# New VectorE durations in the table that paces a hybrid decoder layer's background work

## The chip, the cores and the metric

One core of a Trainium2 chip runs the whole program. The metric is device microseconds (us): the median of three runs of the kernel before is 3039.61 us (3038.51 to 3039.74). A difference under 0.2%, some 6 us, can't be told from no change.

## The reference

One layer of a hybrid decoder over 1024 prompt tokens, and the same layer for one token of each of 8 samples, 2048 wide:

```
h = RMSNorm(x) * (1 + scale(c)) + shift(c)
P = h @ W_in                                  # u, z_s5, r, k, v, w, a, z_rw, two gates
o_s5: S5, 64 groups of 64 complex states:  X_t = a * X_{t-1} + B u_t ;  y = Re(C X) + D u
      y = gelu(y);  o_s5 = y * sigmoid(y @ w_glu + b_glu) * silu(z_s5)
o_rw: 16 heads of 64, a matrix state S:
      S = S * diag(decay) - (S kk) b^T + v k^T ;  o = S r
      o = groupnorm(o) + (r . k * r_k) v ;  o_rw = o * silu(z_rw)
mixed = sigmoid(g_s5) * (o_s5 @ W_out[:1024]) + sigmoid(g_rw) * (o_rw @ W_out[1024:])
x = x + gate(c) * mixed;  y = RMSNorm(x)
```

## The kernel before

**Foreground.** The large products are a list of jobs of 128 output rows. A job of W_in has 3 groups of columns of 48 matmuls each (16 blocks of the contraction, three f16 products for each, L453), 144 in all. Each group fills one of three PSUM buffers (pg) and is evacuated by VectorE: by L517 for r, k, v and w, by L553 for z_s5, by L568 for z_rw. The jobs stand in this order: eight for u, eight for z_s5, then w and a, then k, v, r and z_rw of a pair of heads, for eight pairs, with three jobs for the output gates between one pair's r and its z_rw, and at the end the rest of the gates, the GLU and the 16 output jobs. From the second pair on a turn is seven jobs: k, v, r, three gate jobs, z_rw.

**Background.** The rest is written as generators that stand in a list: the weights' scaling and splitting into two f16 parts (L157, L403, L404), the S5 system (L1127 to L1310), and for each pair of heads
- *operands* (rw_job, L651 to L742): elementwise work, and last eight blocks of masked products, each of 8 matmuls L737 and of four VectorE instructions L739 to L742, a *set* below; then they write to dA in DRAM;
- *inverse* (tinv): dA is loaded, 63 steps of two VectorE instructions each (L798, L800), and the result goes through DRAM to TT;
- *chain*: 16 steps, one after the other, of 7 matmuls: L826, L827, L837 for the inputs, then L834, then L839 and L840; between them XS (L828), UB (L835), S (L842) and ON (L845) on VectorE;
- *tail* (L861 to L157 omx): groupnorm and gate of the chain's output, and the write to od. It needs Z, which the pair's z_rw job fills.

**What sets the order.** Each generator yields three numbers with every step: VectorE ns, TensorE ns and a gap until it is due again. Driver keeps two clocks, pe and ve. After every 8 large matmuls, and after every evacuation, slot() advances pe by these and ve by what the evacuation returned, and lets a generator step while it is due and ve is at most 800 ns ahead of pe, six times at most. Larger numbers thus put fewer steps between the same large matmuls. Where a job needs something that isn't emitted yet, force() emits all that is missing at once, with no large matmul between: job.need for z_rw (it needs the chain and the tail of the pair before), the S5 system ahead of the w job, and the last chain ahead of the first job behind the pairs. A list scheduler then places the emitted instructions on each engine, and may pull large matmuls that are ready a little forward. An engine runs its instructions in that order.

## Time and profile before

| what | value |
|---|---|
| median of three runs | 3039.61 us |
| profiled execution | 3042.96 us, its span 3041.2 us |
| mean granted TensorE clock | 0.959 of full speed |
| TensorE (PE) matmuls busy | 2743.5 us, 90% of the span |
| VectorE (DVE) busy | 2028.4 us, 67%, 4892 instructions |
| ScalarE (ACT), GpSimd (POOL) busy | 984.4 us (32%), 461.2 us (15%) |
| chain that ended last | PE 40%, DVE 28%, DMA 19%, ACT 4% |

PE's busy time is of pipelined matmuls whose ends are modelled. The 2743.5 us leave 297.7 us in which no matmul runs. The inverses of the eight pairs begin at 797.4, 999.7, 1197.1, 1407.9, 1617.0, 1824.1, 2032.3 and 2244.1 us.

### The profile page before, as it was taken

How to read it: one execution, taken by the hardware profiler on the slowest of the kernel's cores; microseconds unless marked ns; L12 is line 12 of the kernel's file. 1: busy time of each engine (PE TensorE's matmuls, PEld its weight loads, DVE VectorE, ACT ScalarE, POOL GpSimd, SP SyncE). 2: the span in 40 equal slices, each digit the busy share in tenths (PEclk: the TensorE clock that was granted, in tenths of full speed). 3: DMA queues.
4: the chain of work that ended last, by engine and by line, in shares of the span. 5: the costliest groups of instructions: out<-in, count | busy, mean ns of one | idle time of the engine just before them, and what ended most of it. 6: DMA issues, size and time to landing. Idle time of an engine off the chain costs nothing.

```text
span 3041.2 us, 47546 instructions
## 1 busy us (share of the span) xinstructions
PE 2743.5 (90%) x18330; PEld 1819.4 (60%) x18330; DVE 2028.4 (67%) x4892; ACT 984.4 (32%) x1734; POOL 461.2 (15%) x749
## 2 busy tenths in 40 slices
PE   5699998999989999899899998998998985899997
PEld 1166666666656666566576675665665653566665
DVE  5579878744675766867767658568566495655555
ACT  2143213324342243243242332432431132422321
POOL 2100000010111112121021111111210222111213
PEclk6799999999999999999999999999999997999998
DMA  9734343331321223213212231232133163664453
GB/s 337 257 80 97 73 86 79 89 97 43 68 66 47 64 67 78 63 51 75 59 52 75 53 81 55 57 78 68 45 80 80 45 210 120 206 203 135 133 146 126
DMA packets 434163, 298.38 MB, mean 98 GB/s; under 512 B 115120, under 2 KB 400464, under 8 KB 432656
## 3 DMA queue, kind: packets, MB, share of 16 engines
q1 hardware_dynamic: 397648, 277.71, 32.9%
q10 hardware_dynamic: 36128, 17.33, 2.1%
q8 instruction: 144, 2.36, 0.3%
q14 instruction: 83, 0.68, 0.1%
q0 software_dynamic: 160, 0.30, 0.0%
HBM read 241.93 MB, written 53.35 MB: 97 GB/s over the span
## 4 chain that ended last, share of the span: by engine, by line
PE 40%; DVE 28%; DMA 19%; ACT 4%; issue 4%; POOL 2%; SPq 1%; ACTq 0%; POOLq 0%; DVEq 0%
PE pg L453 28%; DMA ws<-w_in 7%; DVE TM L798 4%; DVE ZB L800 4%; DMA od<-BV 4%; DVE wlo L404 3%; DVE wam L157 3%; DMA wa<-w_ada 3%; DMA sg<-sgd 2%; PE pma L737 2%; PE up L840 1%; ACT whi L403 1%; PE sp L839 1%; PE up L834 1%; PE pmod L236 1%
## 5 line engine op out<-in xcount | busy, mean ns | idle before, releaser
L453 PEld LDWEIGHTS <-whi 128*128 128x128 f16 x9600 | 943.8, 99 | 571.5 <-issue 109.1
L453 PE MATMUL pg<-H,whi 128*128 128x344 f16 (+2 forms) x3840 | 1200.6, 313 | 66.6 <-DVE ZB L517 38.3
L453 PE MATMUL pg<-H,wlo 128*128 128x344 f16 (+2 forms) x3840 | 1200.9, 313 | 0.0
L453 PE MATMUL pg<-HL,whi 128*128 128x344 f16 (+2 forms) x3840 | 1200.3, 313 | 0.0
L453 PEld LDWEIGHTS <-wlo 128*128 128x128 f16 x4800 | 475.4, 99 | 243.2 <-issue 16.9
L403 ACT ACTIVATE whi<-ws,wsc 128x512 f16<-128x512 f32 x404 | 265.8, 713 | 490.0 <-DVE wsc L150 268.9
L157 DVE TENSOR_REDUCE wam<-ws 128x1 f32<-128x512 f32 x404 | 266.8, 680 | 157.5 <-DMA ws<-w_in 106.5
L404 DVE SCALAR_TENSOR_TENSOR wlo<-ws,wsc,whi 128x512 f16<-128x512 f32 x404 | 301.7, 776 | 57.5 <-ACT whi L403 54.3
L453 PE MATMUL pg<-OH,whi 128*128 128x344 f16 (+3 forms) x960 | 301.0, 314 | 22.0 <-ACT whi L403 10.2
L453 PE MATMUL pg<-OLo,whi 128*128 128x344 f16 (+3 forms) x960 | 301.1, 314 | 3.2 <-DVE OLo L1422 3.2
L453 PE MATMUL pg<-OH,wlo 128*128 128x344 f16 (+3 forms) x960 | 300.9, 313 | 1.0 <-DVE wlo L404 1.0
L798 DVE TENSOR_TENSOR TM<-ZB 128x252 f32<-128x252 f32 (+52 forms) x504 | 179.0, 355 | 88.2 <-DMA ZB<-c_t 77.9
L800 DVE TENSOR_TENSOR ZB<-ZB,TM 128x252 f32<-128x252 f32 (+52 forms) x504 | 179.8, 357 | 10.5
L154 POOL PARTITION_ALL_REDUCE wg<-wm x105 | 50.3, 480 | 865.2 <-DVE wm L157 422.7
L831 POOL TENSOR_SCALAR SG<-S,GC 128x128 f32<-128x128 f32 x120 | 98.6, 821 | 358.5 <-DVE S L842 221.7
L829 ACT COPY XR<-xp 64x128 f32<-64x128 f32 x128 | 33.1, 259 | 351.4 <-DVE XS L828 335.1
L236 PE MATMUL pmod<-wa,cs 128*32 128x512 f32 x256 | 76.7, 866 | 39.1 <-DMA wa<-w_ada 27.6
L842 DVE SCALAR_TENSOR_TENSOR S<-sp,GC,SG 128x128 f32<-128x128 f32 x120 | 41.6, 347 | 73.5 <-POOL SG L831 38.1
L1505 DVE SCALAR_TENSOR_TENSOR sg<-pg,oinv,sg 128x344 f32<-128x344 f32 (+3 forms) x96 | 54.8, 571 | 47.6 <-PE pg L453 47.5
L701 ACT COPY BT<-ZB 64x128 f32<-64x128 f32 x256 | 75.3, 296 | 33.6 <-PE pma L737 24.3
L834 PE MATMUL up<-XS,TT 128*128 128x128 f32 x256 | 56.7, 304 | 30.8 <-DMA TT<-dT 16.9
L147 DVE TENSOR_SCALAR p2m<-wg 128x1 f32<-128x1 f32 x105 | 15.9, 151 | 102.0 <-POOL wg L154 101.1
(443 smaller groups left out, 3223.0 us busy)
## 6 DMA issues: line engine op xcount, KB each, us to landing
ws<-w_in SPq DMA_DIRECT2D x162, 512.0 KB
wa<-w_ada SPq DMA_DIRECT2D x64, 512.0 KB
sg<-sgd SPq DMA_DIRECT2D x32, 516.0 KB
gw<-w_ada ACTq DMA_DIRECT2D x32, 512.0 KB
ws<-w_out SPq DMA_DIRECT2D x32, 512.0 KB
XT<-xT SPq DMA_DIRECT2D x16, 516.0 KB
xo<-xT SPq DMA_DIRECT2D x16, 516.0 KB
ZB<-dA SPq DMA_DIRECT2D x8, 1024.0 KB
```

The lines of the kernel that those rows point to most:

```text
L157: self.nc.vector.tensor_reduce(out=out, in_=in_, axis=axis, op=ALU.max, apply_absolute_value=True)
L236: self.nc.tensor.matmul(q[s:s + 32], cs[:, kt, :], w[:, i, :], start=(kt < 4), stop=(kt >= 12))
L403: nc.scalar.activation(out=hi[:, ks, :], in_=s, func=AF.Copy, scale=job.sc[:, 0, 0:1])
L404: nc.vector.scalar_tensor_tensor(out=lo[:, ks, :], in0=s, scalar=job.sc[:, 0, 0:1], in1=hi[:, ks, :], op0=ALU.mult, op1=ALU.subtract)
L453: nc.tensor.matmul(q[:, :w], a[:, wk, :], b[:, rk, g0:g1], start=(n == 0), stop=(n == tot - 1))
L701: self.nc.scalar.copy(self.BT[k % 2][i][64 * h:64 * h + 64, :, 64 * h:64 * h + 64], t[64 * h:64 * h + 64, 128 * k:128 * k + 128].rearrange ...
L737: nc.tensor.matmul(q[:, e, 128 * i:128 * i + 128], w[:, e, :], self.AR[:, a, 128 * e:128 * e + 128], start=True, stop=True)
L798: nc.vector.tensor_tensor(out=TM, in0=row.unsqueeze(1).to_broadcast([128, n, m]), in1=TL[:, :n, k:k + 1].to_broadcast([128, n, m]), op=ALU ...
L800: nc.vector.tensor_tensor(out=TL[:, :n, k + 1:], in0=TL[:, :n, k + 1:], in1=TM, op=ALU.subtract)
L831: nc.gpsimd.tensor_scalar(out=self.SG, in0=S0, scalar1=g, scalar2=None, op0=ALU.mult)
L834: nc.tensor.matmul(up[:, 0, :], self.TT[:, a, :], xs, start=True, stop=True)
L1505: V.scalar_tensor_tensor(out=f, in0=q[:, :g1 - g0], scalar=job.inv[:, w:w + 1], in1=f, op0=ALU.mult, op1=ALU.mult)
```

## The change

Only the numbers that generators yield and evacuations return are changed, most of them upward. No instruction is added, removed or changed. The core of the diff, with the lines that follow it named in words:

```diff
@@ weights: one block of the split (a scan 600 -> 715, the scale 300 -> 790)
-                yield (620, 0, 0)
+                yield (785, 0, 0)
@@ evacuations: L517 (z_s5 900 -> 1150, z_rw 450 -> 605)
-            return 450.0
+            return 610.0 + (255.0 if g1 == NC else 0.0)
@@ operands: a set of masked products (elementwise steps 1150 -> 1260 to 1440)
-            yield (840, 872, 0)
+            yield (1280, 872, 0)
@@ inverse: one of 63 steps
-            yield (2 * (66 + n * m) / 0.96, 0, 0)
+            yield (2 * (200.0 + n * m), 0, 0)
@@ chain: three yields of one of 16 steps
-            yield (200, 436, CG[0])
+            yield (325, 436, CG[0])
...
-            yield (200, 436, CG[1])
+            yield (325, 436, CG[1])
...
-            yield (400, 436, CG[2])
+            yield (710, 436, CG[2])
@@ tail: half of the groupnorm's scale (other steps 600 to 1200 -> 720 to 1410)
-                yield (680, 872, 0)
+                yield (1030, 872, 0)
@@ S5: powers, runs (1600 -> 2830), fix (2000 -> 2500), scan (560 -> 1220), out (1200 -> 1320)
-        yield (1150, 0, 0)
+        yield (167 + 136 * nt, 0, 0)
```

Three places show what this moves. The first is VectorE's order at the end of the z_rw job of the third turn (job 36), before. Here the masked sets are done; L883 (behind them), L886 and omx are the tail, L798 and L800 the next inverse, and the last row is the first evacuation of z_rw.

```order
L763 STREAM_TRANSPOSE ON<-ZB 128x1024
L886 SCALAR_TENSOR_TENSOR BV<-BV,c_vec,Z 128x1024
L404 SCALAR_TENSOR_TENSOR wlo<-ws,wsc,whi 128x512
L157 TENSOR_REDUCE omx<-BV 128x1
L404 SCALAR_TENSOR_TENSOR wlo<-ws,wsc,whi 128x512 x2
L798 TENSOR_TENSOR TM<-ZB 128x63
L404 SCALAR_TENSOR_TENSOR wlo<-ws,wsc,whi 128x512
L800 TENSOR_TENSOR ZB<-ZB,TM 128x63
L763 STREAM_TRANSPOSE ON<-ZB 128x1024
L798 TENSOR_TENSOR TM<-ZB 128x62
L800 TENSOR_TENSOR ZB<-ZB,TM 128x62
L568 SCALAR_TENSOR_TENSOR Z<-pg,winv,Z 128x344
```

The same place on VectorE in the changed kernel, from the tail's L886 on:

```order
L886 SCALAR_TENSOR_TENSOR BV<-BV,c_vec,Z 128x1024
L739 TENSOR_TENSOR ZB<-pma,c_mat 128x64
L740 TENSOR_TENSOR ZB<-pma,c_mat 128x64
L741 TENSOR_TENSOR M<-pma,c_mat 128x192
L742 TENSOR_TENSOR M<-pma,c_mat 128x192
L157 TENSOR_REDUCE omx<-BV 128x1
L568 SCALAR_TENSOR_TENSOR Z<-pg,winv,Z 128x344 x3
L763 STREAM_TRANSPOSE BV<-ZB 128x1024
L763 STREAM_TRANSPOSE ON<-ZB 128x1024
```

The sets have moved behind the chain's end and into the tail, seven of them after the chain's last instruction (L845), and all three evacuations of z_rw stand behind them.

The second place is TensorE's order at the masked products (L737) of the same turn, before; L453 rows are large matmuls and their weight loads.

```order
L737 MATMUL pma<-AR,BT_5261 128x128
L737 MATMUL pma<-AR,BT_5262 128x128 x2
L737 MATMUL pma<-AR,BT_5261 128x128
L453 LDWEIGHTS whi
L453 MATMUL pg<-HL,whi 128x344
L737 MATMUL pma<-AR,BT_5263 128x128
L737 MATMUL pma<-AR,BT_5264 128x128 x2
L737 MATMUL pma<-AR,BT_5263 128x128
L453 LDWEIGHTS wlo
L453 MATMUL pg<-H,wlo 128x344
```

In the changed kernel they stand between two groups, with the tail's L880 and the next operands' L651, and the last rows are the next job's first large matmul:

```order
L880 MATMUL pmo<-c_mat,ON 128x128 x4
L737 MATMUL pma<-AR,BT_5261 128x128
L737 MATMUL pma<-AR,BT_5262 128x128 x2
L737 MATMUL pma<-AR,BT_5261 128x128
L737 MATMUL pma<-AR,BT_5263 128x128
L737 MATMUL pma<-AR,BT_5264 128x128 x2
L737 MATMUL pma<-AR,BT_5263 128x128
L651 MATMUL pml<-LW,LW_5275 128x344 x2
L453 LDWEIGHTS whi
L453 MATMUL pg<-H,whi 128x347
```

In that run of instructions stand 28 L737, 8 L880, 3 L778 and 2 L651, and no large matmul.

The third place is TensorE's order at the end of the last chain, before: one step with large matmuls between its parts.

```order
L834 MATMUL up<-XS_5269,TT 128x128
L453 LDWEIGHTS whi
L453 MATMUL pg<-HL,whi 128x344
L453 LDWEIGHTS wlo
L453 MATMUL pg<-H,wlo 128x344
L453 LDWEIGHTS whi
L453 MATMUL pg<-H,whi 128x344
L839 MATMUL sp<-UB,BN 128x128
L840 MATMUL up<-UB,M 64x128
L453 LDWEIGHTS whi
L453 MATMUL pg<-HL,whi 128x344
```

In the changed kernel, up to the first large matmul of the job behind the pairs:

```order
L826 MATMUL xp<-S_5266,AR 128x128
L827 MATMUL xp<-VN,M 128x128
L837 MATMUL sp<-VN,KN 128x128
L834 MATMUL up<-XS_5269,TT 128x128
L839 MATMUL sp<-UB,BN 128x128
L840 MATMUL up<-UB,M 64x128
L880 MATMUL pmo<-c_mat,ON 128x128 x8
L453 LDWEIGHTS whi
L453 MATMUL pg<-H,whi 128x344
```

Six steps of the chain stand so, without a large matmul between, and the tail's L880 follow at once.

## Rows read from the trace of the kernel before

**Rows 1.** Windows by stage: length, busy PE, PEld, DVE, ACT, POOL, PEclk, DMA share, GB/s

```profile
174.30:716.50 542.20, 508.47 (x3457) 352.94 (x3457) 392.78 (x883) 164.84 (x275) 34.47 (x80) 0.97 0.37 86
...
966.10:2227.90 1261.80, 1180.67 (x7807) 804.98 (x7805) 872.96 (x2294) 437.99 (x847) 209.47 (x370) 0.99 0.25 64
2227.90:2433.90 206.00, 184.07 (x1238) 124.31 (x1236) 123.10 (x325) 45.96 (x88) 27.49 (x41) 0.97 0.26 69
2433.90:2600.00 166.10, 125.72 (x861) 81.61 (x861) 120.06 (x190) 54.07 (x79) 37.49 (x33) 0.87 0.50 161
```

**Rows 2.** Windows of one turn, from one inverse's start to the next's

```profile
1617.00:1688.00 71.00, 63.80 (x423) 41.75 (x421) 64.24 (x180) 15.81 (x29) 8.45 (x22) 1.00 0.17 48
1688.00:1701.10 13.10, 8.58 (x58) 5.31 (x56) 7.10 (x13) 5.64 (x11) 1.08 (x5) 0.99 0.79 161
1701.10:1785.90 84.80, 83.68 (x539) 57.76 (x540) 52.15 (x127) 34.83 (x61) 16.55 (x27) 0.98 0.18 51
1785.90:1798.50 12.60, 12.45 (x96) 10.11 (x96) 10.27 (x43) 7.88 (x26) 1.72 (x4) 1.00 0.06 19
1798.50:1824.10 25.60, 25.60 (x180) 17.52 (x178) 10.62 (x16) 7.77 (x13) 6.03 (x4) 1.00 0.54 126
```

**Rows 3.** Waits of PE, whole span: waiting line, releaser, us, times, longest

```profile
PE pg L453 <- DVE ZB L517: 38.3, 24, 3.6
...
PE pg L453 <- DVE Z L568: 14.4, 9, 3.5
```

**Rows 4.** Groups of VectorE instructions, 1590 to 1830 us: busy, mean ns, idle before

```profile
L404 DVE SCALAR_TENSOR_TENSOR wlo<-ws,wsc,whi 128x512 f16<-128x512 f32 x32 | 23.9, 768 | 4.6 <-ACT whi L403 4.6
L800 DVE TENSOR_TENSOR ZB<-ZB,TM 128x204 f32<-128x204 f32 (+31 forms) x65 | 23.6, 363 | 1.3
...
L883 DVE SCALAR_TENSOR_TENSOR BV<-pmo,c_vec,BV 128x256 f32<-128x256 f32 x8 | 3.3, 479 | 5.4 <-PE pmo L880 5.4
L741 DVE TENSOR_TENSOR M<-pma,c_mat 128x192 f32<-128x192 f32 x9 | 3.1, 348 | 0.0
...
L869 DVE TENSOR_REDUCE gvr<-pmq 128x8 f32<-128x512 f32 x4 | 2.7, 686 | 0.3
L886 DVE SCALAR_TENSOR_TENSOR BV<-BV,c_vec,Z 128x1024 f32<-128x1024 f32 x2 | 2.5, 1244 | 0.0
...
L739 DVE TENSOR_TENSOR ZB<-pma,c_mat 128x64 f32<-128x64 f32 x9 | 2.0, 223 | 2.3 <-PE pma L737 2.3
```

**Rows 5.** Groups of PE instructions, 1785.9 to 1798.5 us, columns as above

```profile
L737 PE MATMUL pma<-AR,BT 128*128 128x128 f32 x64 | 8.7, 282 | 0.1
```

**Rows 6.** Timeline of PE, one step of the last chain: start, length, instruction

```profile
2408.04 0.38 PE L834 MATMUL up<-XS,TT 128*128 128x128 f32 x2
...
2408.80 0.49 PE L839 MATMUL sp<-UB,BN 128*128 128x128 f32 x2
...
2409.59 0.32 PE L453 MATMUL pg<-HL,whi 128*128 128x344 f16 x1
...
2410.04 0.31 PE L453 MATMUL pg<-HL,whi 128*128 128x344 f16 x1
2410.18 0.38 PE L826 MATMUL xp<-S,AR 128*128 128x128 f32 x2
...
2411.18 0.49 PE L834 MATMUL up<-XS,TT 128*128 128x128 f32 x2
```

**Rows 7.** Timeline of VectorE, the same step

```profile
2409.40 0.35 DVE L842 SCALAR_TENSOR_TENSOR S<-sp,GC,SG 128x128 f32<-128x128 f32 x1 [0.65 <-PE sp L839]
```

**Rows 8.** GpSimd's part of the tail, first lines on the line L872

```profile
L872 POOL TENSOR_TENSOR gvr<-gvr,c_mhalf x8: 2943/2952/3379, 977.4 to 2422.1; 128x16 f32<-128x16 f32 x8
```

**Rows 9.** Groups of VectorE instructions of S5, 560 to 730 us, columns as above

```profile
L1131 DVE TENSOR_TENSOR CB<-CB,CBw 128x1152 f32<-128x1152 f32 x2 | 2.7, 1359 | 0.1
...
L1243 DVE TENSOR_TENSOR X<-X,sfix 128x420 f32<-128x420 f32 x2 | 1.2, 590 | 0.0
```

More of the change, by code (lines that the diff above doesn't have):

```diff
@@ L380, in wscale @@
                 self.absmax(am[:, 2 * h + q:2 * h + q + 1], job.ws[h][:, 4 * q:4 * q + 4, :], axis=mybir.AxisListType.XY)
-                yield (600, 0, 0)
+                yield (715, 0, 0)
         m1 = self.sm.tile([128, 1], F32, name="wm1", tag="wm1")
@@ L385, in wscale @@
         self.gmax(g, m1)
-        yield (100, 0, WGAP)
+        yield (190, 0, WGAP)
         job.sc = self.sm.tile([128, 2, 1], F32, name="wsc", tag="wsc", bufs=3)
@@ L389, in wscale @@
         job.known = True
-        yield (300, 0, 0)
+        yield (790, 0, 0)
     def wsplit(self, job):
@@ L556, in evac @@
             nc.sync.dma_start(self.zsd[b, :, g0:g1], t[:, :w])
-            return 900.0
+            return 1150.0
         return self.job_h(1024 + 128 * b, evac)
@@ L571, in evac @@
                 self.flags.add(f"z{p}")
-            return 450.0
+            return 605.0
         return self.job_h(OFF_RWZ + 128 * p, evac, need=need)
@@ L658, in rw_prep @@
                 if i % 2:
-                    yield (680, 0, 0)
+                    yield (900, 0, 0)
             KQ, SS = self.z(4), self.z(5)
@@ L666, in rw_prep @@
                 V.tensor_scalar(out=SS[:, g0:g1], in0=q[:, :g1 - g0], scalar1=1e-24, scalar2=None, op0=ALU.max)
-                yield (430, 578, 0)
+                yield (550, 578, 0)
             nc.scalar.activation(out=smp[:, 1, :], in_=SIG[:, T:TS], func=AF.Exp, scale=-CDEC)
@@ L670, in rw_prep @@
             self.rsqrt(SS, RN, TQ)
-            yield (2300, 0, 0)
+            yield (2530, 0, 0)
             GI, G = self.z(4), self.z(3)
@@ L677, in rw_prep @@
             V.scalar_tensor_tensor(out=KKN, in0=K, scalar=col("k_k"), in1=RN, op0=ALU.mult, op1=ALU.mult)
-            yield (1150, 0, 0)
+            yield (1320, 0, 0)
             V.tensor_tensor(out=BA, in0=KKN, in1=AA, op=ALU.mult)
-            yield (1150, 0, 0)
+            yield (1320, 0, 0)
             nc.scalar.activation(out=KP, in_=AA, func=AF.Identity, scale=col("k_a"), bias=col("k_a1"))
             V.tensor_tensor(out=KP, in0=KP, in1=K, op=ALU.mult)
-            yield (1150, 0, 0)
+            yield (1320, 0, 0)
             V.scalar_tensor_tensor(out=K, in0=R, scalar=col("r_k"), in1=KP, op0=ALU.mult, op1=ALU.mult)
-            yield (1150, 0, 0)
+            yield (1320, 0, 0)
             V.tensor_tensor(out=BA[:, :T], in0=BA[:, :T], in1=GI[:, :T], op=ALU.mult)
-            yield (1150, 0, 0)
+            yield (1260, 0, 0)
             V.tensor_tensor(out=KP[:, :T], in0=KP[:, :T], in1=GI[:, :T], op=ALU.mult)
-            yield (1150, 0, 0)
+            yield (1260, 0, 0)
             for k in range(2):
@@ L728, in rw_operands @@
             V.tensor_tensor(out=AR4[:, 4 * h:4 * h + 4, 1:3, :], in0=v4(R)[:, 4 * h:4 * h + 4], in1=v4(G)[:, 4 * h:4 * h + 4], op=ALU.mult)
-            yield (1200, 0, 0)
+            yield (1440, 0, 0)
         MA = self.z(3)[:, :T].rearrange("p (c t) -> p c t", t=64)
@@ L763, in rw_side @@
                 V.transpose(out=W, in_=self.z(t)[:, :T])
-                yield (1150, 0, 0)
+                yield (1275, 0, 0)
                 W3 = W.rearrange("p (c b j) -> p c b j", c=16, b=2)
@@ L779, in rw_side @@
                 V.tensor_tensor(out=self.BV[:, g0:g1], in0=q[:, :g1 - g0], in1=Vv[:, g0:g1], op=ALU.mult)
-                yield (450, 578, PBG)
+                yield (545, 578, PBG)
             nc.gpsimd.tensor_copy(self.SMP[:, 6, p, :], self.BV[:, T:TS])
@@ L862, in rw_tail @@
             V.tensor_scalar(out=mu, in0=mu, scalar1=1.0 / 64, scalar2=None, op0=ALU.mult)
-            yield (1200, 0, 0)
+            yield (1410, 0, 0)
             V.tensor_tensor(out=ON, in0=ON, in1=mu.unsqueeze(2).to_broadcast(sh), op=ALU.subtract)
-            yield (1150, 0, 0)
+            yield (1270, 0, 0)
             for b in range(2):
@@ L869, in rw_tail @@
                 V.tensor_reduce(out=vr[:, 8 * b:8 * b + 8], in_=q, axis=AX, op=ALU.add)
-                yield (600, 0, 0)
+                yield (720, 0, 0)
             V.tensor_scalar(out=vr, in0=vr, scalar1=1.0 / 64, scalar2=GN_EPS, op0=ALU.mult, op1=ALU.add)
             nc.gpsimd.tensor_tensor(out=vr, in0=vr, in1=c["mhalf"].to_broadcast([128, 16]), op=ALU.pow)
-            yield (80, 0, 3500)
+            yield (190, 0, 3500)
             V.tensor_tensor(out=ON, in0=ON, in1=vr.unsqueeze(2).to_broadcast(sh), op=ALU.mult)
-            yield (1150, 0, OGAP)
+            yield (1265, 0, OGAP)
             O5 = self.BV[:, :T].rearrange("p (b a e t) -> p b a e t", b=2, a=4, e=2)
@@ L883, in rw_tail @@
                     V.scalar_tensor_tensor(out=o, in0=q[:, :, 1 - e, :], scalar=c["gn_w"][:, p:p + 1], in1=o, op0=ALU.mult, op1=ALU.add)
-                yield (680, 872, 0)
+                yield (1030, 872, 0)
             O = self.BV[:, :T]
             V.scalar_tensor_tensor(out=O, in0=O, scalar=c["gn_b"][:, p:p + 1], in1=self.Z[:, :T], op0=ALU.add, op1=ALU.mult)
-            yield (1150, 0, 0)
+            yield (1285, 0, 0)
             self.absmax(self.omx[:, p:p + 1], O)
@@ L890, in rw_tail @@
             self.flags.add(f"o{p}")
-            yield (1150, 0, 0)
+            yield (1245, 0, 0)
     def rw_sample(self):
@@ L1127, in s5_powers @@
         V.tensor_tensor(out=o, in0=e(e1), in1=f(self.PR), op=ALU.mult)
-        yield (1150, 0, 0)
+        yield (167 + 136 * nt, 0, 0)
         V.tensor_tensor(out=w, in0=e(e2), in1=f(self.PI), op=ALU.mult)
-        yield (1150, 0, 0)
+        yield (167 + 136 * nt, 0, 0)
         V.tensor_tensor(out=o, in0=o, in1=w, op=op)
-        yield (1150, 0, 0)
+        yield (167 + 136 * nt, 0, 0)
         return o
@@ L1158, in s5_prep @@
         tt(b2, b2, t[:, 0], ALU.subtract)
-        yield (1300, 0, 0)
+        yield (1950, 0, 0)
         BB = yield from self.s5_powers(b, "BB", b1, b2, 8, ALU.add)
@@ L1207, in s5_inj @@
                         nc.vector.tensor_copy(o, q[64 * ri:64 * ri + 64])
-                yield (350, 460, 0)
+                yield (480, 460, 0)
     def s5_runs(self, q):
@@ L1227, in s5_runs @@
                 V.tensor_tensor(out=o[r], in0=o[r], in1=T[:, r], op=ALU.add)
-            yield (1600, 0, 0)
+            yield (2830, 0, 0)
     def s5_fix(self, b):
@@ L1243, in s5_fix @@
             V.tensor_tensor(out=o, in0=o, in1=T1, op=ALU.add)
-            yield (2000, 0, 0)
+            yield (2500, 0, 0)
     def s5_scan(self):
@@ L1257, in s5_scan @@
             V.tensor_tensor(out=X[:, :, :, k], in0=X[:, :, :, k], in1=T1, op=ALU.add)
-            yield (560, 0, 0)
+            yield (1220, 0, 0)
         s8 = [128, 2, 32, NS]
@@ L1272, in s5_scan @@
             nc.gpsimd.dma_start(d["o_s5s"][r], A1[:, r])
-        yield (2500, 0, 0)
+        yield (4500, 0, 0)
     def s5_tg(self, b):
@@ L1295, in s5_out @@
                     nc.scalar.copy(o, i)
-        yield (1200, 0, 3000)
+        yield (950, 0, 3000)
         Y = self.U[:, 8 * b:8 * b + 8, 0:136]
@@ L1313, in s5_out @@
             self.s5_tg(b + 2)
-        yield (1200, 0, 0)
+        yield (1320, 0, 0)
     def s5_main(self):
```

## The prediction

> **What bounds the kernel now.** I read first the windows by stage. In each row the length less PE's busy time is the time in which no matmul runs. In the six full turns it is 1261.80 - 1180.67 = 81.1 us, and the clock stands at 0.99; in the stage behind the last chain it is 166.10 - 125.72 = 40.4 us at 0.87 [rows 1]. Since the change touches no instruction, PE's work stays as it is, and the question is only how this idle time changes. VectorE is busy for 872.96 of the 1261.80 us, so it has room as a mean.
>
> Then I read one turn in pieces, from the start of one pair's inverse to that of the next [rows 2]. It is a closed chain of dependences: the inverse 71.0, its way through DRAM 13.1, the sixteen steps of the chain 84.8, the masked products of the next pair 12.6, dA's way through DRAM 25.6, together 207.1 us. PE is busy for 63.80 + 8.58 + 83.68 + 12.45 + 25.60 = 194.1 of them, so 13.0 us are idle. The turn is thus held nearly as much by this ring as by PE's work: a few us more in the ring and PE must wait for it, since its instructions stand in a fixed order and the chain's L834 blocks the large matmuls behind it. Last I read what PE waits for: evacuations, 38.3 us on L517 and 14.4 us on L568 [rows 3]. These waits come where VectorE has a queue of background work in front of an evacuation, and such queues are what new VectorE durations can shorten or lengthen.
>
> **What the change does.** With larger durations fewer steps are emitted between the same large matmuls, and as the number of steps and of jobs is the same, more is left when a job needs it, and is forced out at once. The printed order shows this at each z_rw job from the second pair on: the last step of the chain, the tail and seven sets of masked products now stand without a large matmul between, in front of z_rw's evacuations.
>
> *The bunch, on VectorE.* Behind the chain's last instruction and before the first L568 stand seven sets of about 1.14 us (two instructions of 223 ns and two of 348), three L404 of 768 ns, four L883 of 479, two L869 of 686, and six instructions over 1024 columns, for which I take 1244 ns each (L861, L864, L874, L763, L886, omx) [rows 4]. That is 8.0 + 2.3 + 1.9 + 1.4 + 7.5 = 21.1 us. All three pg buffers hold z_rw's groups by then, so the next job's first large matmul waits for the first L568. GpSimd's 2.95 us between L871 and L874 [rows 8] lies beside two sets and an L404, some 3.0 us, and costs nothing; without these it would.
>
> *The bunch, on PE.* In that time PE has 27 large matmuls, 28 L737 at 8.7 / 64 = 0.136 us [rows 5], and 13 others of at most 0.4 us. A large matmul takes (2410.04 - 2409.59) / 3 = 0.15 us [rows 6]. That makes 4.0 + 3.8 + about 3 = 10.8 us, so 10 us of each bunch are idle.
>
> *The wait for the inverse.* Counted in the changed order, 608 large matmuls lie between the bunch and the first L834 of the next chain (about 650 between the masked products and there before). They take 91 us, and with 4 us of small ones PE has 95 us of work. The ring needs 25.6 for dA, the inverse, and 13.1 for TT. The inverse itself: 71.0 us now, of which VectorE is busy for 64.24 [rows 2]; the other instructions that stand within it come to 26.6 us in place of 28.6, so I take 69. That is 107.7 us, and 13 us of PE idle. Together 10 + 13 = 23 us of idle time for each turn in place of 13.0: +10.
>
> *The ring, as a second count.* 25.6 + 69 + 13.1, the chain, and the bunch up to its last set, 21.1 - 1.2 = 19.9 in place of 12.6. In the chain stand 376 large matmuls where 334 stood: up to 42 x 0.15 = 6.3 us more. Small matmuls of the operands that lay there go ahead of it, so I take 2 us, with 0 and 6.3 as bounds: 86.8. The ring is 214.4 us, +7.3. Between the two counts I take +8 for each of six turns: 48 us. For the first turn, whose next pair meets the same bunch but which had more idle time of its own, I take half, 4 us, with 0 and 10 as bounds.
>
> *The last turn.* Before, 206.00 - 184.07 = 21.9 us are idle [rows 1]. After, the wait for the inverse (13) stays, and the last six steps of the chain stand alone. Such a step lasts from L834 to L839 0.76, from there to the end of S 2409.75 - 2408.80 = 0.95, and from L826 to the next L834 1.00, some 2.75 us [rows 6, 7]; PE's own part is 3.14 - 10 x 0.15 = 1.64, since ten large matmuls lie in the 3.14 us. So 6 x 1.1 = 6.7 us are idle. Then L880 waits for the tail: three instructions of 1.24, two of 0.69 and GpSimd's 2.95, 8.0 us [rows 4, 8]. Together 27.7 in place of 21.9: +6.
>
> *S5.* 79 steps are forced in front of the w job, where before the background had run dry by then. VectorE has there 48 instructions of the state's correction at 590 ns and 18 of powers at 1359 ns [rows 9], 28.3 + 24.5, and with the transposes, maxima and splits some 87 us; PE has about 72 us of ready work, 288 large matmuls and 256 small ones. So 15 to 20 us are idle. But the same work costs idle time before too, spread over the stage's 542.20 - 508.47 = 33.7 us [rows 1]. I take +4; the bounds are -15, if nearly all of it goes, and +20, if all of it stays.
>
> *Weights, evacuations, output.* Their larger numbers act through the same bunches; on their own I cost them at nothing, since L157 and L404 are emitted in time for the job after next, behind a whole job of 21 us. If that cover is gone, each such job waits for a split of some us.
>
> *The clock.* In the turns 1% of 1261.80 us, some 12.6 us, goes with 81.1 us of idle time: 0.15 us for each us [rows 1]. The 62 us above bring 9 more; the upper bound is the stage with 0.87, 0.13 x 166.10 / 40.4 = 0.53, that is 33.
>
> **The sum** is 48 + 4 + 6 + 4 + 9 = 71 us on the profiled execution's 3042.96. That execution lies 3.35 us above the median of three runs, so the forecast is 3110.6, rounded to 3111 us. By the ends of its terms (six turns of +5 to +11, S5 -15 to +20, the clock 5 to 33) its own range is 3070 to 3155.
>
> **Rivals.**
> *The clock falls at each bunch.* The bunch is 21 us with PE half idle, and then comes a second wait of 13 us. If PE drops to its lower level (1.2 GHz) there as in the stage with 0.87, each idle us costs 0.53 more, and the count of +10 holds for seven turns: (70 + 6 + 4) x 1.53 = 122, or 3162 us. For it speaks that stage; against it that the turns have waits now and keep 0.99. The Trainium skill ("TensorE: Matmul & The Clock Gate", section "HAM oscillation — how this bites in real kernels") says that a loop whose every pass has a wait can lose the full clock in every pass and pay the warm-up each time. By that rule this rival would be the likeliest, at 3162; the row with 0.99 beside 81 us of waits speaks against it so far.
>
> *No change.* PE's 90% busy time stays as it is, and the idle time only moves from evacuations to bunches: 3040 us. Against it stands that the ring of 207.1 us has no room for seven more us. [...]
>
> *Faster.* With true durations VectorE's queue in front of evacuations gets short, and the 38.3 + 14.4 us of waits [rows 3] shrink. With half of them gone the time is 3013 us, with all of them 2987. It decides if the forced bunches fall beside waits that are there anyway, that is if the wait at z_rw costs under 4 us for each turn. For it speaks that the old numbers are below the measured ones (a set 840 against 1.14 us); against it that the largest of these waits, at z_rw, is the place where the bunch now stands.
>
> **How the numbers follow.** The forecast has 70%, the falling clock 14%, no change 7%, faster 9%. Slower by over 0.2% (6 us, about what a measurement of this kernel can tell from no change) is the sum of the first two, 0.84; within 0.2% 0.07; faster 0.09. The range from 3050 to 3170 leaves out the faster case, most of no change, and the upper part of the falling clock.
>
> **What would show it.** In the profile after, PE's wait on L568 should grow from 14.4 us to some 70; the wait of L834 for TT should grow to some 80 us; a turn, from one inverse to the next, should last 214 to 218 us, with L739 to L742 behind the chain's last L845; the six last steps of the chain should each take about 2.75 us. The prediction is wrong if the wait on L568 stays under 30 us, if the inverse takes well under 69 us, since then the ring has room again, or if the granted clock in the turns falls below 0.96.

## The result, and the profile after

| | before | changed |
|---|---|---|
| median, four runs each | 3039.06 us | 3171.66 us (3168.84 to 3173.34) |
| span of the profiled execution | 3041.2 us | 3171.6 us |
| granted clock, whole span | 0.959 | 0.943 |

The ratio is 1.0434, 95% interval 1.0418 to 1.0451: slower, as forecast, but by 133 us where 71 were forecast, just above the range's end of 3170.

The page of the changed kernel, section 1: busy time of each engine, its share of the span, instructions.

```profile
PE 2770.6 (87%) x18330; PEld 1838.3 (58%) x18330; DVE 2019.9 (64%) x4892; ACT 978.8 (31%) x1729; POOL 474.1 (15%) x749
```

PE does the same 18330 matmuls, busy for 2770.6 us in place of 2743.5. So of the 130.4 us in the span, 27.1 are longer matmuls, read here as the same work at a lower clock, and 103.3 are idle time.

Where it lies is read from the starts of the inverses. The first starts at 834.7 us (before 797.4): +37.3 us ahead of the turns. The last starts at 2376.3 (2244.1): the seven turns between take 1541.6 us in place of 1446.7, +94.9. From there to the end it is 795.3 against 797.1 us. But the inverse itself moves among the jobs: the first starts 69 large matmuls later in their list than before, the last 193 later. So the loss is read a second time between the same large matmuls (the 2882nd, 4178th, 10226th and 11089th of 14400). The stages are the start, the jobs up to the end of S5, the first pair's jobs with the first turn, six full turns, the last turn, and the rest. Before, columns as in [rows 1]:

```profile
0.00:174.30 174.30, 113.85 (x470) 36.76 (x471) 109.52 (x272) 51.76 (x59) 29.03 (x31) 0.77 0.76 260
174.30:716.60 542.30, 508.57 (x3457) 353.02 (x3457) 392.78 (x883) 164.91 (x276) 34.47 (x80) 0.97 0.37 86
716.60:997.40 280.80, 258.02 (x1673) 174.27 (x1671) 178.93 (x456) 116.57 (x218) 39.39 (x79) 0.97 0.26 61
997.40:2249.00 1251.60, 1173.24 (x7759) 799.16 (x7758) 863.90 (x2266) 431.12 (x826) 206.45 (x369) 0.99 0.25 64
2249.00:2434.00 185.00, 163.04 (x1094) 110.19 (x1092) 113.64 (x310) 36.98 (x73) 23.21 (x36) 0.96 0.23 64
2434.00:3041.20 607.20, 526.76 (x3884) 345.95 (x3883) 369.64 (x707) 183.04 (x284) 128.61 (x154) 0.94 0.52 160
```

The same in the changed kernel:

```profile
0.00:174.30 174.30, 109.30 (x483) 35.63 (x484) 111.22 (x275) 51.75 (x59) 28.92 (x31) 0.86 0.78 264
174.30:743.60 569.30, 504.56 (x3446) 350.51 (x3444) 393.00 (x880) 150.87 (x264) 44.68 (x80) 0.96 0.35 81
743.60:1032.30 288.70, 261.79 (x1676) 177.56 (x1675) 182.12 (x468) 118.30 (x218) 38.96 (x81) 0.96 0.23 58
1032.30:2353.10 1320.80, 1195.40 (x7785) 814.05 (x7784) 859.15 (x2263) 439.96 (x835) 211.21 (x367) 0.96 0.23 60
2353.10:2568.60 215.50, 167.76 (x1063) 113.00 (x1061) 115.82 (x320) 35.76 (x70) 22.05 (x38) 0.88 0.24 65
2568.60:3171.60 603.00, 531.82 (x3884) 347.54 (x3883) 358.63 (x689) 182.12 (x284) 128.26 (x153) 0.94 0.51 159
```

The stage up to the end of S5 grows by 27.0 us, the first turn by 7.9, the six turns by 69.2 (11.5 each), and the last turn by 30.5; the rest gives back 4.2.

One turn of the changed kernel in the pieces of [rows 2]:

```profile
1716.60:1787.00 70.40, 55.52 (x341) 35.32 (x339) 61.87 (x180) 16.17 (x30) 7.77 (x17) 0.90 0.17 50
1787.00:1804.20 17.20, 17.20 (x113) 11.24 (x111) 8.73 (x23) 9.00 (x11) 0.59 (x2) 1.00 0.51 127
1804.20:1889.10 84.90, 83.74 (x573) 58.59 (x572) 46.19 (x115) 25.44 (x51) 16.84 (x30) 1.00 0.16 47
1889.10:1909.70 20.60, 15.95 (x100) 12.64 (x99) 17.17 (x46) 11.89 (x30) 5.59 (x3) 0.92 0.10 29
1909.70:1934.60 24.90, 23.68 (x147) 15.13 (x148) 9.15 (x15) 10.06 (x18) 4.79 (x11) 0.93 0.54 122
```

Against [rows 2] the inverse is as long (70.40 for 71.0), but PE is idle for 14.9 us of it in place of 7.2, at a clock of 0.90. The way from the inverse's end to the first L834 is 17.20 for 13.1, the chain as long as it was, and from the chain's last L840 to dA's write (L749) it is 20.60 for 12.6. Over six turns the clock is 0.96 where it was 0.99.

What PE waits for in the changed kernel, whole span, as in [rows 3]:

```profile
PE pml L651 <- ACT ZB L652: 66.5, 7, 11.4
...
PE pg L453 <- ACT whi L403: 27.5, 10, 8.5
PE pmo L880 <- DVE ON L874: 25.8, 8, 9.6
PE pg L453 <- DVE ZB L517: 23.9, 11, 5.4
PE xp L826 <- DVE S L842: 23.8, 12, 10.3
PE pg L453 <- ACT gt__5386 L587: 15.1, 1, 15.1
PE pg L453 <- DVE LW L517: 13.4, 1, 13.4
...
PE pg L453 <- DVE Z L568: 6.9, 7, 2.7
```

The waits on L517 for ZB and on L568 have shrunk, from 38.3 and 14.4; one of 13.4 us on L517 for LW, in S5, is new. The wait of L834 for TT, 16.9 us in six waits before, is gone. Largest is now 66.5 us at L651, the first matmul of the next pair's operands, once in each turn; before it was 10.0 us in two waits.

### The profile page after: what moved, and what is told of

The parts are those of the page before. It is cut to its first block, busy times and chain, and to the rows that moved or that the text cites. A ratio compares the mean times of both kernels' runs of the same rounds, so it can differ in the third digit from the quotient of the medians.

```text
span 3171.6 us, 47603 instructions
## 1 busy us (share of the span) xinstructions
PE 2770.6 (87%) x18330; PEld 1838.3 (58%) x18330; DVE 2019.9 (64%) x4892; ACT 978.8 (31%) x1729; POOL 474.1 (15%) x749
## 4 chain that ended last, share of the span: by engine, by line
PE 43%; DVE 24%; DMA 18%; issue 7%; ACT 5%; POOL 3%; SPq 1%; ACTq 0%; POOLq 0%; DVEq 0%
PE pg L453 31%; DMA ws<-w_in 11%; DVE TM L798 3%; DVE ZB L800 3%; DVE wlo L404 3%; DVE wam L157 2%; DMA wa<-w_ada 2%; DMA sg<-sgd 1%; PE up L840 1%; PE sp L839 1%; ACT whi L403 1%; PE pma L737 1%; PE up L834 1%; DMA gw<-w_ada 1%; PE pmod L236 1%
## 5 line engine op out<-in xcount | busy, mean ns | idle before, releaser
L453 PEld LDWEIGHTS <-whi 128*128 128x128 f16 x9600 | 943.2, 99 | 592.5 <-issue 122.0
L453 PE MATMUL pg<-H,whi 128*128 128x344 f16 (+2 forms) x3840 | 1201.6, 313 | 87.6 <-DVE ZB L517 23.9
L453 PE MATMUL pg<-H,wlo 128*128 128x344 f16 (+2 forms) x3840 | 1201.3, 313 | 1.2 <-DVE wlo L404 1.2
L453 PE MATMUL pg<-HL,whi 128*128 128x344 f16 (+2 forms) x3840 | 1200.7, 313 | 0.0
L453 PEld LDWEIGHTS <-wlo 128*128 128x128 f16 x4800 | 476.2, 99 | 243.1 <-issue 11.7
L403 ACT ACTIVATE whi<-ws,wsc 128x512 f16<-128x512 f32 x404 | 266.0, 712 | 457.9 <-DVE wsc L150 322.4
L404 DVE SCALAR_TENSOR_TENSOR wlo<-ws,wsc,whi 128x512 f16<-128x512 f32 x404 | 303.2, 773 | 82.6 <-ACT whi L403 81.0
L453 PE MATMUL pg<-OH,whi 128*128 128x344 f16 (+3 forms) x960 | 301.6, 314 | 17.9 <-ACT whi L403 15.0
L453 PE MATMUL pg<-OLo,whi 128*128 128x344 f16 (+3 forms) x960 | 301.7, 314 | 0.0
L453 PE MATMUL pg<-OH,wlo 128*128 128x344 f16 (+3 forms) x960 | 301.2, 314 | 0.4 <-DVE wlo L404 0.3
L798 DVE TENSOR_TENSOR TM<-ZB 128x252 f32<-128x252 f32 (+52 forms) x504 | 176.4, 350 | 124.4 <-DMA ZB<-c_t 113.4
L800 DVE TENSOR_TENSOR ZB<-ZB,TM 128x252 f32<-128x252 f32 (+52 forms) x504 | 175.9, 349 | 11.0 <-DVE TM L798 0.4
L831 POOL TENSOR_SCALAR SG<-S,GC 128x128 f32<-128x128 f32 x120 | 88.8, 740 | 358.3 <-DVE S L842 174.0
L842 DVE SCALAR_TENSOR_TENSOR S<-sp,GC,SG 128x128 f32<-128x128 f32 x120 | 41.8, 348 | 132.6 <-POOL SG L831 107.2
L651 PE MATMUL pml<-LW,LW 128*128 128x344 f32 x96 | 44.6, 583 | 76.5 <-ACT ZB L652 66.5
L737 PE MATMUL pma<-AR,BT 128*128 128x128 f32 x512 | 80.0, 308 | 12.3 <-ACT BT L701 6.7
L737 PEld LDWEIGHTS pma<-AR,BT 128*128 128x128 f32 x512 | 72.5, 217 | 23.9 <-ACT BT L701 15.1
```

The costliest lines, as they stand in the source:

```text
L403: nc.scalar.activation(out=hi[:, ks, :], in_=s, func=AF.Copy, scale=job.sc[:, 0, 0:1])
L404: nc.vector.scalar_tensor_tensor(out=lo[:, ks, :], in0=s, scalar=job.sc[:, 0, 0:1], in1=hi[:, ks, :], op0=ALU.mult, op1=ALU.subtract)
L453: nc.tensor.matmul(q[:, :w], a[:, wk, :], b[:, rk, g0:g1], start=(n == 0), stop=(n == tot - 1))
L651: nc.tensor.matmul(q[:, :g1 - g0], self.LW2[:, w, :], self.LW[:, g0:g1], start=True, stop=True)
L737: nc.tensor.matmul(q[:, e, 128 * i:128 * i + 128], w[:, e, :], self.AR[:, a, 128 * e:128 * e + 128], start=True, stop=True)
L798: nc.vector.tensor_tensor(out=TM, in0=row.unsqueeze(1).to_broadcast([128, n, m]), in1=TL[:, :n, k:k + 1].to_broadcast([128, n, m]), op=ALU ...
```

## What holds TensorE at L651

ScalarE's timeline in the changed kernel, in the turn above: start, length, instruction, idle time before it and its releaser.

```profile
1754.29 1.95 ACT L403 ACTIVATE whi<-ws,wsc 128x512 f16<-128x512 f32 x3
1756.26 0.99 ACT L511 ACTIVATE mt<-pg,rinv 128x347 f32<-128x347 f32 x2
1771.95 0.72 ACT L403 ACTIVATE whi<-ws,wsc 128x512 f16<-128x512 f32 x1 [14.70 <-DVE wsc L150]
...
1773.14 0.98 ACT L652 ACTIVATE ZB<-pml,c_vec 128x344 f32<-128x344 f32 x2
```

PE at the same time:

```profile
1763.01 1.32 PE L651 MATMUL pml<-LW,LW 128*128 128x344 f32 x4
...
1773.74 2.66 PE L651 MATMUL pml<-LW,LW 128*128 128x344 f32 x4 [9.11 <-ACT ZB L652]
```

Two L651 fill the two PSUM buffers of their kind; the third waits until ScalarE has emptied one. ScalarE has that L652 behind an L403, and L403 has waited 14.70 us for a weight's scale (L150), which VectorE computes between the steps of the inverse, with an all-reduce on GpSimd in the middle. So PE, with more than a hundred large matmuls behind L651, stands still for a weight scale. Before, ScalarE has the same wait in the inverse, up to 19.0 us, but L651 comes only within the next chain, and no matmul of this turn hangs on it. This is read from the trace; the experiments below do not isolate it.

## What holds it in S5

SyncE's queue in the changed kernel, ahead of the w job:

```profile
581.92 3.79 SPq L1280 DMA_DIRECT2D D<-KRd  x8
603.96 5.76 SPq L1311 DMA_DIRECT2D yd<-U  x8
609.82 4.35 SPq L1280 DMA_DIRECT2D D<-KRd  x8
614.27 1.21 SPq L1138 DMA_DIRECT2D Ct<-Cs  x2
615.53 0.59 SPq L589 DMA_DIRECT2D sgd<-gt__5334  x1
```

And PE's three longest waits there:

```profile
618.61 0.45 PE L453 MATMUL pg<-H,whi 128*128 128x347 f16 x1 [15.12 <-ACT gt__5386 L587]
...
657.49 0.79 PE L1302 MATMUL pmy<-XRt,CB 128*128 128x136 f32 x2 [7.74 <-DVE CB L1131]
...
677.14 0.45 PE L453 MATMUL pg<-H,whi 128*128 128x347 f16 x1 [13.41 <-DVE LW L517]
```

The write of a gate (sgd, L589) stands behind 18 DMAs of the forced S5 steps, of which those of L1311 wait for the S5 output. The gate's buffer is free only after it: ScalarE's L587 waits 11.58 us for this write, and PE stands for 15.12 us. The stretch from 593 to 677 us has 84 us with 45 us of PE work, at a clock of 0.79.

## The experiments

The kernel before took 3022 to 3026 us on the chips of these runs, so ratios are compared; the changed kernel is 1.0434. The table under the experiments has the ring of twelve kernels.

**All but S5** (the numbers of L1128 to L1314 as before).

> The changed kernel with the S5 system's numbers as before. The trace of the changed kernel has the w job 27 us later than before, and the first inverse 37 us later. Theory 1 (the forced S5 steps cost this): 3135 to 3145 us, and the job behind w begins at 650 to 655 us. Rival (the delay at the w job is given back by later work, as the stages behind it have waits of their own): 3160 to 3172 us.

1.0365 (1.0334 to 1.0396). The first inverse starts at 802.2 us in place of 834.7; the turns stay long. The ratio lies between the two expectations, which are 1.031 to 1.035 and 1.040 to 1.044 of the kernel before. S5 is some 0.7%, 21 us, of the loss in the median, and 32 us by the start of the first inverse.

**S5 alone** (only those lines new).

> The kernel before with only the S5 system's numbers new. Theory 1: 27 to 37 us slower, 3066 to 3076 us, with the wait of TensorE for a gate job's evacuation (L587) that the changed kernel has. Rival (it needs the new weights' numbers too, since these bring the forced steps from 58 to 89): 3040 to 3055 us.

1.0122 (1.0096 to 1.0147), 37 us. By the traces the first inverse starts 27.5 us later than in the kernel before. The turns are as before. But its wait is not the expected one: 23.7 us on the evacuation of w (L517), none on L587. The mechanism in S5 has two ends, VectorE's row and SyncE's.

**S5's DMAs off SyncE.**

```diff
-            self.nc.sync.dma_start(self.D[b % 2][...], self.KRd[...])
+            self.nc.scalar.dma_start(self.D[b % 2][...], self.KRd[...])
...
-                nc.sync.dma_start(yv[t], self.U[...])
+                nc.scalar.dma_start(yv[t], self.U[...])
```

> The changed kernel with the S5 blocks' writes to yd and their loads of D issued by ScalarE in place of SyncE. In the changed kernel TensorE waits 15.1 us for a gate evacuation, whose buffer waits for its write, and that write stands on SyncE behind these DMAs. Theory 4 (SyncE's order costs it): the wait is under 3 us, the w job's end 10 to 15 us earlier, 1.038 to 1.040 of the kernel before. Rival (VectorE's row of forced S5 steps ends last anyway): the wait moves to the evacuation of w (L517, 13.4 us now), 1.042 to 1.045.

1.0403 (1.0376 to 1.0430). The wait on L587 is gone. In that stretch PE now waits like this:

```profile
PE pmy L1302 <- ACT U L1304: 24.0, 6, 12.1
PE pg L453 <- DVE LW L517: 10.9, 1, 10.9
```

The job's length falls from 84.1 to 72.5 us, but it starts 8.3 us later, so it ends only 3.4 us earlier (expected 10 to 15). The first inverse starts 8 us earlier. In the median 9 us are gained, with intervals that overlap: that SyncE's order costs this much is likely, not shown. That the rest is the forced steps waiting for each other is read from the traces and was not tested.

**All but the inverse, and the inverse alone** (`2 * (66 + n * m) / 0.96` for `2 * (200.0 + n * m)`, and the reverse).

> The changed kernel with the inverse's numbers as before. In its order the masked products and the tail have large matmuls between again, and the last large matmul ahead of L834 of the next chain comes later. Theory 2 (the inverse's larger numbers push the chain to the turn's end, and so make the bunch and the wait at L651): seven turns shorter by 7 to 12 us, 3090 to 3125 us. Rival (all VectorE numbers together exceed the budget, and each of them alone is enough): 3155 to 3172 us.

> The kernel before with only the inverse's numbers new. In its order eight L737, three L778 and two L651 of a turn stand without a large matmul between, half of the changed kernel's bunch, and L651 stands ahead of the chain. Theory 2: 3070 to 3110 us, most of what the turns lose in the changed kernel. Rival: 3039 to 3055 us.

1.0385 (1.0353 to 1.0416) without it, 1.0403 (1.0371 to 1.0434) with it alone. Theory 2 falls as it was put: the inverse's numbers are enough for nearly the whole loss, and without them nearly as much is lost.

**The debt forgiven**, in the changed kernel and in the kernel before.

```diff
                 if cond():
-                    return
+                    self.ve = min(self.ve, self.pe + self.slack); return
```

> The changed kernel, with ve cut back to pe + 800 at the end of each force(). All new numbers stay. Theory 3 (the numbers do their harm through a debt: forced steps are charged to ve, which then stands up to 30 us ahead of pe, and slot() lets no background step, the chain's included, until pe has caught up): most of the turns' loss goes, 1.00 to 1.02 of the kernel before. Rival (the harm is done in slot() itself, where each step now waits longer): 1.03 to 1.045.

> The kernel before with ve cut back to pe + 800 at the end of each force(). It has forced steps too, up to 27 at once, and a debt of 9 us at most. Theory 3: 0.99 to 1.003 of the kernel before, and the wait of the chain for the inverse gets shorter. Rival (its order is as good as the table can make it): 1.00 to 1.01.

1.0276 (1.0249 to 1.0303) and 1.0166 (1.0136 to 1.0196). With the new numbers it gives back half of each turn's loss (213.7 for 220.2 us), with the old ones it costs 10 us a turn. Both ratios lie outside both expectations. The debt is a part of it, but having none isn't good in itself: theory 3 fails as a rule.

**All numbers times 0.9, 0.8, 0.7** (`self.ve = max(...) + 0.8 * v`, and the same in slot()).

> The changed kernel with every VectorE number, evacuations too, times 0.8 in the clock ve. The proportions among the steps are the new ones; the sum of a turn is 139 us of VectorE where the changed kernel counts 172, the kernel before 124 and its trace shows 145 busy. Theory 3 (it is the sum that counts, as it makes the debt): 0.995 to 1.012 of the kernel before. Rival (the new proportions put the steps of the chain and of the masked products in bad places): 1.02 or more.

> The changed kernel with every VectorE number times 0.9 in the clock ve; a turn counts 155 us of VectorE, and the inverse is forced again with 31 and 27 steps in a turn where 0.8 has at most 15. Theory 6 (the loss has an edge, where the steps between two deadlines no longer fit and are forced): 1.025 to 1.042 of the kernel before, near the changed kernel. Rival (the loss grows evenly with the numbers, 1.0034 at 0.8 and 1.0434 at 1): 1.018 to 1.025.

> The changed kernel with every VectorE number times 0.7; a turn counts 124 us, as in the kernel before, and no inverse step is forced. In its order the chain begins later than at 0.8, up to some 140 large matmuls later in the turn. Theory 6 (below the edge the numbers hardly matter): 0.997 to 1.006 of the kernel before. Theory 7 (the ring): the way from the inverse's end to the first L834 grows to 20 us or more, 1.01 to 1.03.

0.9: 1.0473 (1.0456 to 1.0491); 0.8: 1.0034 (1.0018 to 1.0050); 0.7: 1.0506 (1.0482 to 1.0529). At 0.8 theory 3's expectation is met, at 0.9 theory 6's is exceeded, and at 0.7 neither holds. No edge and no slope: 0.8 is a valley between two slow orders. At 0.7 no inverse is forced, yet the turns take 223.3 us, with dA's write 36.0 us behind the chain. Neither expectation for 0.7 had this: theory 7 had looked for a late L834, which stayed at 15.2.

**The inverse uncharged** (`yield (0, 0, 0)` in its step).

> The changed kernel with the inverse's steps charged at 0: no inverse is forced any more, a turn counts 123 us of VectorE, as the kernel before (124). But in its order the last two steps of a chain, the next pair's L651 and L665, nearly all L737 and the tail stand without a large matmul between, at each z_rw job. Theory 7 (the ring is what counts, and the bunch at z_rw is its largest growth): the way from the chain's last L840 to dA's write is 25 us or more, a turn 215 to 230 us, 1.03 to 1.06 of the kernel before. Rival (the forced inverse steps are the cause, by what they delay behind them): the turns are back at 205 to 211 us, 1.010 to 1.02.

1.0796 (1.0769 to 1.0823). Without any forced inverse step the turns are the longest of all, 234.5 us, with 46.8 us from the chain's end to dA's write. The forced inverse steps as such are not the cause of slow turns. Theory 7 had the direction; turn and ratio lie above its ranges.

**The inverse's inputs moved** (L1 at z4 and z5, L2 at z0), in three kernels. Here the transposes that fill BN stand behind the load into z5 and read its words, so BN isn't the layer's; instructions and sizes are the same.

> The changed kernel, with the inverse's inputs L1 and L2 in the buffers z4, z5 and z0 in place of z0, z1 and z4, so that SIG (z1) and AA (z2) of the next pair can be written while an inverse runs. In the changed kernel TensorE waits 66.5 us, seven times, for L652, which writes SIG. Theory 5 (this wait holds the large matmuls that stand ahead of the next chain, and so delays its first L834): the wait is under 15 us, from the inverse's end to the first L834 it takes 13 to 15 us in place of 17.7, 1.030 to 1.038 of the kernel before. Rival (the wait passes to L834, which waits for TT, and the ring stays as long): 1.040 to 1.046.

> The same move of L1 and L2, with all new VectorE numbers times 0.8. It may beat the kernel before: with 0.8 alone TensorE still waits 27.1 us for L652. Theory 5: this wait goes and the time is 0.990 to 1.000 of the kernel before. Rival (at 0.8 the ring has room, the wait is paid elsewhere): 1.000 to 1.006.

> The kernel before with the same move of L1 and L2. Its wait for L652 is 10.0 us in all. Theory 5: 0.995 to 1.001. Rival (the load of dA into z5 now waits for the transposes that read it, and the ring grows): 1.003 to 1.015.

1.0345 (1.0328 to 1.0363), 1.0005 (0.9990 to 1.0020), 0.9934 (0.9915 to 0.9953). The first is 0.9% off the changed kernel: the wait for L652 falls from 66.5 to 6.7 us, and the first L834 comes 15.2 us behind the inverse in place of 17.7. But the order has changed too, five L651 stand in the bunch now. With this wait nearly gone a turn still takes 215.0 us in place of 206.7, so it isn't shown that the wait at L651 by itself makes the turns slow. At 0.8 PE waits 27.1 us there, and the turns are as before. The second ratio lies at the border of its two expectations, the third below both.

**SIG's buffer alone** (SIG in z5, SS in z1, RN in z5; the layer's own result).

> The kernel before, with SIG of the next pair in z5, and the sum and its root (SS, RN) in each other's buffers z1 and z5; L1 and L2 stay where they are, and all numbers stay. z5 is free from the pair's first transpose on, z1 only from the inverse's 32nd step on. The run with L1 and L2 moved gave 0.9934, and its way from the inverse's end to the first L834 was 12.9 us in place of 15.1. Theory 5 (it was SIG's buffer that held TensorE there): 0.990 to 0.997, with this way under 14 us. Rival (the gain came from the moved load, which is not here): 0.998 to 1.002.

> The same buffers for SIG, SS and RN with all new VectorE numbers times 0.8. With 0.8 alone TensorE waits 27.1 us for L652. Theory 5: that wait is under 12 us, 0.993 to 1.001 of the kernel before. Rival: 1.001 to 1.005, as with 0.8 alone.

> The same buffers for SIG, SS and RN with the changed kernel's numbers. The run with L1 and L2 moved gave 1.0345 in place of 1.0434. Theory 5: 1.030 to 1.038, the wait for L652 under 25 us in place of 66.5. Rival (AA's part of L652 or PSUM's two buffers hold TensorE as long): 1.040 to 1.046.

1.0005 (0.9990 to 1.0020), 1.0023 (1.0004 to 1.0043), 1.0441 (1.0411 to 1.0471). Theory 5 falls: with the buffer free PE waits as long at L651. The waits of the last one:

```profile
PE pml L651 <- ACT ZB L652: 71.6, 13, 10.2
```

Its ScalarE stands again 14.69 us at an L403 for L150, with L652 behind. So by the trace the holder is ScalarE's order; a run that takes only L403 out of the way wasn't made, and why the moved inputs helped the kernel before by 0.66% stays open.

**The ring in twelve kernels**, means of seven turns, worked out from the times of the first L798 and last L800 (inverse), the first L834, the last L840 and the first DMA of L749 of each pair:

| kernel | ratio | inverse | to L834 | chain | to dA's write | to next inverse | turn |
|---|---|---|---|---|---|---|---|
| before | 1 | 70.9 | 15.1 | 82.3 | 12.5 | 25.8 | 206.7 |
| S5 alone | 1.0122 | 70.2 | 15.1 | 82.0 | 12.4 | 25.4 | 205.1 |
| 0.8 | 1.0034 | 73.0 | 15.0 | 82.9 | 10.9 | 25.2 | 207.1 |
| new, debt forgiven | 1.0276 | 71.0 | 18.0 | 82.6 | 17.0 | 25.0 | 213.7 |
| new, inputs moved | 1.0345 | 68.4 | 15.2 | 86.2 | 20.3 | 24.7 | 215.0 |
| before, debt forgiven | 1.0166 | 72.3 | 16.8 | 71.8 | 31.0 | 25.0 | 216.9 |
| all but the inverse | 1.0385 | 69.5 | 19.9 | 78.4 | 23.9 | 26.0 | 217.7 |
| changed | 1.0434 | 70.5 | 17.7 | 85.2 | 21.1 | 25.7 | 220.2 |
| 0.9 | 1.0473 | 62.7 | 18.1 | 94.4 | 21.7 | 24.9 | 221.8 |
| 0.7 | 1.0506 | 71.9 | 15.2 | 75.4 | 36.0 | 24.7 | 223.3 |
| inverse alone | 1.0403 | 71.7 | 22.7 | 78.9 | 24.8 | 26.0 | 224.1 |
| inverse uncharged | 1.0796 | 69.8 | 15.1 | 78.6 | 46.8 | 24.3 | 234.5 |

dA's way through DRAM, to the next inverse, is as long in all of them. All orders with a turn of 205 to 207 us have dA's write within 13 us of the chain's end; all others have it 17 us or more behind it. The seven kernels left out fit: four with turns of 203.6 to 206.2 us have it 10.9 to 13.0 us behind the chain, three with 217.4 to 218.5 us have it 20.5 to 21.3 us behind. No version clearly beat the kernel before with the layer's own result.

## Why the prediction was right and wrong

The forecast was 71 us, the measured growth of the span 130.4. The windows between the same large matmuls give each term of the sum; all but the clock's are idle time of PE.

| term | forecast, us | measured, us |
|---|---|---|
| S5 | +4 (-15 to +20) | +31.0 |
| first turn | +4 (0 to 10) | +4.1 |
| six turns | +48 (30 to 66) | +47.0 |
| last turn | +6 | +25.8 |
| start, and what follows the pairs | 0 | +4.6 and -9.3 |
| clock (longer matmuls) | +9 (5 to 33) | +27.1 |

So three terms were mis-sized: S5, the last turn and the clock. The turns had the right size, but from other waits than those that the forecast added up.

*The ring: right in the main.* The inverse, the chain and the masked products follow each other in all kernels, and slow turns go with a late dA's write, as the table of the ring shows. That this lateness is the cause is argued: no run moved the masked products alone. In the changed kernel the link from the inverse to the first L834 isn't TT any more, for which PE no longer waits, but PE's own backlog.

*The bunch: right in length, wrong in what waits.* VectorE's row before the first L568 was put at 21.1 us, and the way to dA's write at 19.9; it is 20.6 us in the turn shown. But the forecast had PE wait behind the bunch, some 70 us on L568; there it waits 6.9. PE's timeline at that place in the changed kernel, waits only:

```profile
1898.35 1.13 PE L737 MATMUL pma<-AR,BT 128*128 128x128 f32 x8 [0.69 <-ACT BT L701]
1901.62 1.08 PE L880 MATMUL pmo<-c_mat,ON 128*128 128x128 f32 x4 [2.15 <-DVE ON L874]
...
1910.22 0.82 PE L651 MATMUL pml<-LW,LW 128*128 128x344 f32 x2 [1.21 <-DVE M L742]
1911.73 0.45 PE L453 MATMUL pg<-H,whi 128*128 128x347 f16 x1 [0.70 <-DVE Z L568]
```

The bunch's own small matmuls wait one by one, mostly for VectorE, so by the time of the next job L568 is nearly done. PE's work in the bunch was put too low as well: 28 L737 at 0.136 us, 3.8 us. But the 64 rows of [rows 5] are 32 instructions, as each L737 stands in the trace with two rows; the bunch has 56 rows, 7.6 us. PE is busy for 15.95 of the 20.60 us, where 10.8 of 21 were forecast, and 4.65 us are idle in place of 10.

*"The wait for the inverse": failed in its place.* 13 us of idle time were put at L834, behind TT, and taken as ending with it. PE waits already at L651, for ScalarE, then has to work off what stands behind, and the first L834 comes 17.7 us after the inverse in place of 15.1. The printed rows had the two L651 at the end of the bunch; that four more of the kind stand within the inverse and need ScalarE, which waits for VectorE's scale first, was not followed up. The wait of L834 for TT, forecast to grow to some 80 us, is none.

*The turns: +8 was right in size, in part by luck.* Six turns have 47.0 us more idle time, 7.8 for each. The forecast's 23 us of idle time in a turn are 21.9 in the turn shown, but 14.9 of them lie within the inverse, with the wait at L651, and none at L834. Counted by the inverses, with the clock's share in it, a turn is 13.5 us longer: 8.6 are between the chain's end and dA's write (forecast 7.3), 2.6 before L834 (forecast 0, as TT's 13.1 were kept), 2.9 in the chain (forecast 2), and the inverse is 0.4 shorter (forecast 2).

*S5: the step that failed most.* "+4, bounds -15 and +20" is 31.0 us of idle time in the changed kernel; with only S5's numbers new the kernel loses 37 us (1.0122), and with S5's old numbers the changed kernel gains 21. It was counted from VectorE's and PE's sums as if the two ran beside each other; VectorE was busy for only 51 of the 84 us. By the trace the forced steps wait for each other on several engines, and their DMAs hold SyncE for the gate's write. The order of SyncE was not looked at.

*The clock: 9 was mis-sized.* PE's matmuls took 27.1 us longer. The turns went from 0.99 to 0.96, although their idle time for each turn only grew from 13 to 21 us. In the six turns 22.2 us of longer matmuls (with 26 more small ones among them) came with 47.0 us of idle time, 0.47 for each: nearer the upper bound of 0.53 than the 0.15 of [rows 1]. Over the whole span it is 27.1 for 103.3, 0.26. In the turn shown the granted clock is at its lower level from 1768.1 us on, within the wait of 9.11 us at L651:

```profile
1768.10:1778.30 10.20, 4.56 (x12) 2.49 (x13) 9.54 (x32) 5.17 (x10) 0.10 (x1) 0.50 0.01 3
```

The Trainium skill ("TensorE: Matmul & The Clock Gate", section "HAM oscillation — how this bites in real kernels") had this: a wait in every pass of a loop can cost the full clock in every pass. The 0.90 to 0.93 in the pieces with the waits agree with it, though two of the five pieces keep 1.00.

*The last turn: mis-sized.* +6 was forecast, from six lone steps with 1.1 us of idle time each and 8.0 us for the tail. Between the same large matmuls it is 25.8 us of idle time, and the turn is 30.5 us longer. PE's waits over 5 us there:

```profile
2532.67 0.77 PE L826 MATMUL xp<-S,AR 128*128 128x128 f32 x2 [6.79 <-DVE S L842]
...
2547.11 0.77 PE L826 MATMUL xp<-S,AR 128*128 128x128 f32 x2 [10.27 <-DVE S L842]
...
2560.91 1.97 PE L880 MATMUL pmo<-c_mat,ON 128*128 128x128 f32 x8 [9.63 <-DVE ON L874]
2568.60 0.44 PE L453 MATMUL pg<-H,whi 128*128 128x344 f16 x1 [5.72 <-ACT gt__21978 L587]
```

The tail's wait, 9.63, was foreseen. Two of the six lone steps wait 6.79 and 10.27 us for S, which waits for GpSimd's SG behind an all-reduce (shown at the end); GpSimd was left out of the forecast's step, and so was the gate's L587.

*Weights: put at nothing.* PE's waits for a weight's split (L403) grew from 15.2 us in two waits to 27.5 in ten, so the cover that the forecast counted on was not always there.

*The rivals.* The falling clock, with 3162 us, came closest, and the clock does fall in the bunch (0.92) and in the inverse with the wait at L651 (0.90); but S5 and L651 were in it no more than in the forecast. No change and faster fell: the waits on L517 for ZB and on L568 did shrink, by 22 us, and this was lost among the others.

## What to carry to other kernels

A table of new durations isn't a better schedule, and its sum no guide: for a turn in which VectorE is busy for 145 us the old table counts 124 and the new one 172. Times 0.8 and 0.9 the new one counts 139 and 155, near the 145, and costs 0.3% and 4.7%. In a planner with deadlines the numbers move whole blocks of work past each other. Here the inverse's numbers alone, all the others without them, and a tenth up or down from 0.8 each cost 4 to 5%. Look for the closed ring of dependences that holds a loop, and tune the order until its links follow each other, whatever numbers give that. When work is forced ahead of a job, follow each of its instructions on every queue, ScalarE's, GpSimd's and SyncE's too: by the traces much of the cost was in what stood behind them. And measure a stage between the same instructions of the bounding engine: counted from the inverse, which had itself moved, the last turn seemed to cost nothing.
